# The first stage of a hybrid block kernel: c spread over partitions by its transfer, x times the first norm's factor by token and transposed a second time, first modulation on ScalarE

## The chip, the cores and the metric

The kernel runs on one core of a Trainium2 chip. The metric is the device time of one execution in microseconds, the median of the runs; lower is better. A core has five engines that run side by side, each through its own instructions in a fixed order: TensorE (PE in the profile, its weight loads PEld), VectorE (DVE), ScalarE (ACT), GpSimd (POOL) and SyncE (SP), which only starts transfers here. Transfers run on 16 DMA engines that all queues share.

## The reference

Two layers with three sub-blocks each (feed-forward, mixer, feed-forward) on x of 256 tokens by 1024, in fp32. Each sub-block begins with a norm that is modulated by a vector c. Only the first one matters here:

```python
c_act = jax.nn.silu(c)
mod = (c_act @ ada_w[layer] + ada_b[layer]).reshape(bsz, N_SUB, 3, D_MODEL)[:, :, :, None, :]

def rms_norm(x, g):
    y = xf * lax.rsqrt(jnp.mean(xf * xf, axis=-1, keepdims=True) + EPS)
    return y * g

def modulate(t, sub):
    return rms_norm(t, norm_g[layer, sub]) * (1.0 + mod[:, sub, 1]) + mod[:, sub, 0]

def swiglu(h, w_gate, w_up, w_down):
    return (jax.nn.silu(h @ w_gate) * (h @ w_up)) @ w_down

h = modulate(x, 0)
x = x + HALF_STEP * (1.0 + mod[:, 0, 2]) * swiglu(h, ...)
```

## The kernel before

Activations are kept with channels on the 128 partitions and the 256 tokens along the row: x is eight chunks of 128 by 256. Weights stream from memory once, in pieces of 128 by 1024, eight tiles each. To keep fp32 accuracy, each piece is split into a high part (a cast on ACT, `whi`, line 88 or 92) and the remainder (a subtraction on DVE, `wlo`, line 93), and each activation chunk likewise (`hb`, its two halves); a product is then three matmuls: high by high (line 309), high weight by low activation (310), low weight by high activation (311). Three buffers hold raw pieces, six the parts, three the raw ada blocks; a load waits on SP until its buffer is free.

In the first sub-block (`s == 0` in `ffn`) the loop runs over the eight chunks k of x on the outside, and for each over eight output blocks j, gate and up. So PE can begin with the first chunk alone: 48 matmuls for a chunk, into eight PSUM banks (four of tag `mm`, two `ax`, one `p`, one `q`). Ahead of that stand:

- **c** (lines 153 to 177): one row of 1024 is loaded from ACT's queue; PE spreads it over the partitions by a product with ones, in two halves of 512, and ACT applies Silu to each half, giving `cact`.
- **x** (lines 155 to 188): two loads on SP's queue, tokens on partitions (`xn`); DVE sums the squares of each half (line 182, with its sum in `ss_in`); PE transposes the sixteen 128 by 128 blocks (line 187), and ACT copies them to `x` (line 188), which is also what the residual adds to later.
- **the modulation** (`ada_block`, lines 199 to 207): each block is a load of 128 by 1024 on SP and a product with `cact` on DVE, summed along the row (line 206). Blocks 0 and 1 give shift and scale of chunk 0, and so on by pairs; those of chunk k + 1 are asked for while chunk k's products are issued. The columns of biases and gains (`cols`, line 451) come by ACT's queue, and `b1` (line 454), `scales` (458) and `shifts` (461) on DVE are made of them.
- **the norm's factor**: `rs_tokens` (263 to 276) makes of the two sums one factor for each token, in twelve small DVE steps (lines 275 and 252 to 259; the inverse root is an integer start and three Newton steps). `rs_bcast` (278 to 285) spreads it with PE to a row that is the same on all partitions, and ACT copies it to `rs`.
- **the chunk** (`modulate_chunk`, 319 to 328): DVE makes `ht`, x times scale times rs (line 323); ACT adds the shift and rounds to the high part (325); DVE makes the low part (326).

The order on each engine is fixed when the kernel is built, by a planner that takes instructions by their place in the program and by when it reckons them ready; it need not be the order of the lines. Some orders are set by hand: `W.first` holds the three instructions of the first chunk's modulation, and the first two weight remainders stand behind its first entry, the second high part behind its second:

```python
if i == 1:
    self.tc.add_manual_dep(raw_hi.ins, self.first[1].ins.name, NOSYNC, reason="the first input first")
...
if i < 2:
    self.tc.add_manual_dep(self.last.ins, self.first[0].ins.name, NOSYNC, reason="the first input first")
```

Of the kernel before, what the change touches and what calls it, by code (L numbers as in the profile page):

```python
# [11 lines left out]
F32 = mybir.dt.float32  # L12
F32R = mybir.dt.float32r
I32 = mybir.dt.int32
AF = mybir.ActivationFunctionType
ALU = mybir.AluOpType
# [3 lines left out]
P = 128  # L20
# [104 lines left out]
def body(ctx: ExitStack, tc: tile.TileContext, a, out, dbg=None):  # L125
# [14 lines left out]
    def mm_bank(name):  # L140
        return ps_mm.tile([P, 512], F32, tag="mm", name=name)
# [8 lines left out]

    first = ExitStack()
    fpool = first.enter_context(tc.tile_pool(name="first", bufs=1, reuse_waits="tile"))
    crow = fpool.tile([1, D], F32, name="crow")
    nc.scalar.dma_start(crow, a["c"])
    xn = fpool.tile([P, 2, D], F32, name="xn")
    nc.sync.dma_start(xn[:, 0], a["x"][0:P, :])
    nc.sync.dma_start(xn[:, 1], a["x"][P:T, :])
# [13 lines left out]
    ones = cst.tile([P, P], F32, name="ones")  # L171
    nc.gpsimd.memset(ones, 1.0)
    cact = cst.tile([P, D], F32, name="cact")
    for i in range(2):
        b = mm_bank(f"c{i}")
        nc.tensor.matmul(b, ones[0:1, :], crow[:, 512 * i:512 * i + 512], start=True, stop=True)
        nc.scalar.activation(cact[:, 512 * i:512 * i + 512], b, AF.Silu)

    ss_in = fpool.tile([P, 2], F32, name="ss_in")
    for b in range(2):  # L180
        q = fpool.tile([P, D], F32, name=f"xsq{b}")
        nc.vector.scalar_tensor_tensor(out=q, in0=xn[:, b], scalar=1.0, in1=xn[:, b], op0=ALU.mult, op1=ALU.mult,
                                       accum_out=ss_in[:, b:b + 1])
    for k in range(0, ND, 2):
        b = mm_bank(f"xT{k}")
        for i in range(4):
# [132 lines left out]
    def modulate_chunk(s, k, rs):  # L319
# [7 lines left out]
                                            in1=h[k][:, 0, :].bitcast(F32), op0=ALU.add, op1=ALU.subtract)  # L327
        return mul, hi, lo

    def scale_shift_columns(s):  # L330
        sh, _ = mod_shift_scale(s)
        shb = sh.unsqueeze(2).to_broadcast([P, 8, 2])
        nc.vector.tensor_copy(hh[:, :, T:T + 2], shb)
        nc.vector.tensor_tensor(out=hl[:, :, T:T + 2], in0=shb, in1=hh[:, :, T:T + 2].bitcast(F32), op=ALU.subtract)
# [93 lines left out]
    def ffn(s, acc, fp, during=None):  # L428
# [11 lines left out]
        if s == 0:  # L440

            done = NF0
            rs = xp.tile([P, T], F32, tag="rs", name="rs0")
            pb = rs_bcast(acc, D, "n0")
            nc.scalar.copy(rs, pb)
            banks = [mm_bank(f"gu0_{j}") if j < 4 else ax_bank(f"gu0_{j}", ("ax", "ax", "p", "q")[j - 4])
                     for j in range(NF0)]
            heads = [None] * NF0
# [8 lines left out]
            for k in range(ND):  # L457
                nc.vector.scalar_tensor_tensor(out=scales[0][:, k:k + 1], in0=mods[0][:, 8 + k:9 + k],
                                               scalar=b1[:, k:k + 1], in1=cols[:, g + k:g + k + 1],
                                               op0=ALU.add, op1=ALU.mult)  # L460
                nc.vector.tensor_tensor(out=shifts[0][:, k:k + 1], in0=mods[0][:, k:k + 1], in1=cols[:, o + k:o + k + 1],
                                        op=ALU.add)
                chain = modulate_chunk(0, k, pb if k == 0 else rs)
                if k == 0:
                    W.first = chain
                for j in range(NF0):
                    for i in range(2):
                        dst = banks[j][:, i * T:(i + 1) * T]

                        m = multiply(dst, h[k], k == 0 and i == 0, k == ND - 1)  # L470
                        if k == 0 and i == 0:
                            heads[j] = m
                        elif k == 0:
                            tc.add_manual_dep(m.ins, heads[j].ins.name, NOSYNC, reason="one start per bank")
                        if j == i == 0 and k + 1 < ND:
                            ada_block(2 * k + 2)
                            ada_block(2 * k + 3)
# [684 lines left out]
```

## Time and profile before

| | us |
|---|---|
| median of 3 runs | 1161.99 |
| lowest and highest | 1160.93, 1162.44 |
| the profiled execution | 1166.55 |
| its span, first to last instruction | 1164.6 |
| PE busy in it | 1139.7 |
| DVE busy in it | 960.0 |
| ACT busy in it | 640.8 |

The profile is of one execution. Its views used here are the page, the list of waits (engine, line, what it waited for: us in total, times, longest), the timeline (start, length, engine, line, operation, output and inputs, count, idle time before it and who ended it), groups by line (count, busy us, mean ns), and windows (length; busy us and count of PE, PEld, DVE, ACT and POOL; the granted clock of PE as a share of full; share of the DMA engines; GB/s). "SPq" and "ACTq" are the queues' issuing instructions.

### The profile page before, as it was taken

How to read it: one execution, taken by the hardware profiler on the slowest of the kernel's cores; microseconds unless marked ns; L12 is line 12 of the kernel's file. 1: busy time of each engine (PE TensorE's matmuls, PEld its weight loads, DVE VectorE, ACT ScalarE, POOL GpSimd, SP SyncE). 2: the span in 40 equal slices, each digit the busy share in tenths (PEclk: the TensorE clock that was granted, in tenths of full speed). 3: DMA queues.
4: the chain of work that ended last, by engine and by line, in shares of the span. 5: the costliest groups of instructions: out<-in, count | busy, mean ns of one | idle time of the engine just before them, and what ended most of it. 6: DMA issues, size and time to landing. Idle time of an engine off the chain costs nothing.

```text
span 1164.6 us, 21862 instructions
## 1 busy us (share of the span) xinstructions
PE 1139.7 (98%) x8526; PEld 1084.3 (93%) x8526; DVE 960.0 (82%) x1838; ACT 640.8 (55%) x1070; POOL 8.8 (1%) x24
## 2 busy tenths in 40 slices
PE   7999999999999999999999998999999999999997
PEld 6999988999988999998899998889999989999986
DVE  7999899999889798778788888979869988666553
ACT  4464444778875564444454354448765466444451
POOL 0000000000000000000000000010000000000000
PEclk8999999999999999999999999999999999999999
DMA  8989989556555568888748899973432475765550
GB/s 324 348 299 359 359 302 325 194 185 199 174 180 176 187 211 324 306 297 297 265 150 308 281 331 344 335 250 101 162 111 73 131 235 160 259 220 189 183 181 37
DMA packets 74985, 272.25 MB, mean 234 GB/s; under 512 B 8417, under 2 KB 8577, under 8 KB 74882
## 3 DMA queue, kind: packets, MB, share of 16 engines
q1 hardware_dynamic: 74016, 268.99, 67.6%
q8 instruction: 67, 1.10, 0.4%
q0 software_dynamic: 432, 1.10, 0.4%
q10 hardware_dynamic: 434, 0.76, 0.2%
q14 instruction: 36, 0.29, 0.1%
HBM read 269.77 MB, written 1.05 MB: 233 GB/s over the span
## 4 chain that ended last, share of the span: by engine, by line
PE 76%; DVE 11%; DMA 7%; ACT 3%; issue 1%; ACTq 0%; DVEq 0%; SPq 0%
PE od L410 16%; PE gu L310 11%; PE gu L311 11%; PE gu L309 11%; PE od L412 8%; DMA wraw<-in_wst_dram 5%; DVE wlo L93 4%; ACT whi L92 2%; DVE ada L206 1%; DMA wgr<-in_ml_wg_dram 1%; PE gu_f L358 1%; PE up L311 1%; PE up L310 1%; PE gu_f L356 1%; PE gu_f L357 1%
## 5 line engine op out<-in xcount | busy, mean ns | idle before, releaser
L92 ACT CAST whi<-wraw 128x1024 fp32r<-128x1024 f32 x364 | 380.4, 1048 | 304.2 <-DMA wraw<-in_wst_dram 151.0
L93 DVE TENSOR_TENSOR wlo<-wraw,whi 128x1024 fp32r<-128x1024 f32 x366 | 446.8, 1221 | 106.7 <-ACT whi L92 105.5
L311 PE MATMUL gu<-hb,wlo 128*128 128x256 f32 x1312 | 371.0, 284 | 0.0
L310 PE MATMUL gu<-hb,whi 128*128 128x256 f32 x1312 | 370.1, 283 | 0.1
L309 PE MATMUL gu<-hb,whi 128*128 128x256 f32 x1312 | 364.6, 282 | 1.5 <-ACT hb L325 1.5
L410 PE MATMUL od<-ph,whi 128*128 128x512 f32 x704 | 247.9, 395 | 3.3 <-DVE ph L303 3.3
L309 PEld LDWEIGHTS gu<-hb,whi 128*128 128x128 f32 x1312 | 248.7, 191 | 1.9 <-ACT hb L325 1.9
L310 PEld LDWEIGHTS gu<-hb,whi 128*128 128x128 f32 x1312 | 248.5, 189 | 0.4 <-DVE hb L326 0.3
L311 PEld LDWEIGHTS gu<-hb,wlo 128*128 128x128 f32 x1312 | 247.7, 189 | 0.0
L412 PE MATMUL od<-ph,wlo 128*128 128x256 f32 x704 | 197.6, 281 | 0.0
L206 DVE SCALAR_TENSOR_TENSOR ada<-ada,cact 128x1024 f32<-128x1024 f32 x144 | 175.0, 1218 | 0.0
L410 PEld LDWEIGHTS od<-ph,whi 128*128 128x128 f32 x704 | 133.0, 189 | 34.7 <-DVE ph L303 3.6
L412 PEld LDWEIGHTS od<-ph,wlo 128*128 128x128 f32 x704 | 132.7, 188 | 0.0
L302 ACT CAST ph<-fg 128x256 fp32r<-128x256 f32 x88 | 35.2, 405 | 87.2 <-DVE fg L437 86.9
L417 DVE SCALAR_TENSOR_TENSOR x<-od,gate,x 128x256 f32<-128x256 f32 x88 | 42.1, 481 | 26.8 <-PE od L412 22.1
L303 DVE TENSOR_TENSOR ph<-fg,ph 128x256 fp32r<-128x256 f32 x88 | 36.6, 421 | 12.6 <-ACT ph L302 12.5
L410 PE MATMUL od<-yb,whi 128*128 128x512 f32 x128 | 45.2, 395 | 0.0
L436 ACT ACTIVATE fg<-gu 128x256 f32<-128x256 f32 x82 | 30.8, 378 | 13.9 <-PE gu L311 13.8
L311 PE MATMUL zz<-hb,wlo 128*128 128x256 f32 x128 | 37.5, 293 | 0.0
L309 PE MATMUL zz<-hb,whi 128*128 128x256 f32 x128 | 37.5, 293 | 0.0
L310 PE MATMUL zz<-hb,whi 128*128 128x256 f32 x128 | 37.1, 290 | 0.0
L293 ACT ACTIVATE sq_o<-x 128x256 f32<-128x256 f32 x42 | 17.4, 415 | 35.1 <-DVE x L417 32.9
(398 smaller groups left out, 1882.8 us busy)
## 6 DMA issues: line engine op xcount, KB each, us to landing
wraw<-in_wst_dram SPq DMA_DIRECT2D x366, 512.0 KB, 4.4
ada<-in_adaT_dram SPq DMA_DIRECT2D x144, 512.0 KB, 5.4
xn<-in_x_dram SPq DMA_DIRECT2D x2, 512.0 KB, 4.0
wgr<-in_ml_wg_dram POOLq DMA_DIRECT2D x3, 256.0 KB, 6.4
out_dram<-res SPq DMA_DIRECT2D x2, 256.0 KB, 3.0
out_dram<-res ACTq DMA_DIRECT2D x2, 256.0 KB, 3.0
cols<-in_cols_dram ACTq DMA_DIRECT2D x1, 226.0 KB, 5.2
wkr<-in_ml_wkr_dram POOLq DMA_DIRECT2D x1, 128.0 KB, 3.5
```

Source lines behind the costliest of these rows:

```text
L92: raw_hi = nc.scalar.copy(hi, raw)
L93: self.last = nc.vector.tensor_tensor(out=lo, in0=raw, in1=hi.bitcast(F32), op=ALU.subtract)
L206: nc.vector.scalar_tensor_tensor(out=raw, in0=raw, scalar=1.0, in1=cact, op0=ALU.mult, op1=ALU.mult, accum_out=mods[s][:, m:m + 1])
L302: nc.scalar.copy(hi, src)
L303: nc.vector.tensor_tensor(out=both[:, 1, :], in0=src, in1=hi.bitcast(F32), op=ALU.subtract)
L309: m = nc.tensor.matmul(dst, wh, both[:, 0, :], start=start, stop=False, skip_group_check=True)
L310: nc.tensor.matmul(dst, wh, both[:, 1, :], start=False, stop=False, skip_group_check=True)
L311: nc.tensor.matmul(dst, wl, both[:, 0, :], start=False, stop=stop, skip_group_check=True)
L410: nc.tensor.matmul(bank, wh, both.rearrange("p i t -> p (i t)"), start=(k == 0), stop=False, skip_group_check=True)
L412: nc.tensor.matmul(sums[0], wl, both[:, 0, :], start=False, stop=(k == len(rhs) - 1), skip_group_check=True)
L417: nc.vector.scalar_tensor_tensor(out=xs_t[d], in0=part, scalar=g[:, d:d + 1], in1=xs_t[d], op0=ALU.mult, op1=ALU.add)
L436: nc.scalar.activation(g, b[:, 0:T], AF.Silu)
```

## The change

c is loaded as 128 copies of its row, 512 KB in place of 4 KB, straight into all partitions; the two products and the two half Silus become one Silu. The second half of x has its squares summed on ACT and not on DVE. The norm's factor is not spread to a row any more: x, with tokens on partitions, is multiplied by it in place (first half on ACT, second on DVE), and transposed a second time into a new tile `xr`, with ACT copying again. The first transposes, into `x`, stay for the residual. A chunk's modulation (`shift_chunk`) is two passes on ACT over `xr`, one rounded to the high part and one not, and one subtraction on DVE. It returns the subtraction first and the high part second, so the first two weight remainders now stand behind the low part.

```diff
-    crow = fpool.tile([1, D], F32, name="crow")
-    nc.scalar.dma_start(crow, a["c"])
+    call = fpool.tile([P, D], F32, name="call")
+    nc.scalar.dma_start(call, a["c"][0:1, :].to_broadcast([P, D]))
...
     cact = cst.tile([P, D], F32, name="cact")
-    for i in range(2):
-        b = mm_bank(f"c{i}")
-        nc.tensor.matmul(b, ones[0:1, :], crow[:, 512 * i:512 * i + 512], start=True, stop=True)
-        nc.scalar.activation(cact[:, 512 * i:512 * i + 512], b, AF.Silu)
+    nc.scalar.activation(cact, call, AF.Silu)
 
     ss_in = fpool.tile([P, 2], F32, name="ss_in")
-    for b in range(2):
-        q = fpool.tile([P, D], F32, name=f"xsq{b}")
-        nc.vector.scalar_tensor_tensor(out=q, in0=xn[:, b], scalar=1.0, in1=xn[:, b], op0=ALU.mult, op1=ALU.mult,
-                                       accum_out=ss_in[:, b:b + 1])
+    junk = [fpool.tile([P, D], F32, name=f"xsq{b}") for b in range(2)]
+    nc.vector.scalar_tensor_tensor(out=junk[0], in0=xn[:, 0], scalar=1.0, in1=xn[:, 0], op0=ALU.mult, op1=ALU.mult,
+                                   accum_out=ss_in[:, 0:1])
+    nc.scalar.activation(junk[1], xn[:, 1], AF.Square, accum_out=ss_in[:, 1:2])
...
+    def shift_chunk(k, src):
+
+        sh, sc = shifts[0], scales[0]
+        hi = nc.scalar.activation(h[k][:, 0, :], src, AF.Identity, bias=sh[:, k:k + 1], scale=sc[:, k:k + 1])
+        t = tmp.tile([P, T], F32, tag="v", name=f"ht0_{k}")
+        nc.scalar.activation(t, src, AF.Identity, bias=sh[:, k:k + 1], scale=sc[:, k:k + 1])
+        lo = nc.vector.tensor_tensor(out=h[k][:, 1, :], in0=t, in1=h[k][:, 0, :].bitcast(F32), op=ALU.subtract)
+        return lo, hi
...
-            rs = xp.tile([P, T], F32, tag="rs", name="rs0")
-            pb = rs_bcast(acc, D, "n0")
-            nc.scalar.copy(rs, pb)
+            rs = rs_tokens(acc, D, "n0")
+            xr = fpool.tile([P, ND, T], F32, name="xr")
+            for k in range(0, ND, 2):
+                w = slice(k * P, (k + 2) * P)
+                nc.scalar.activation(xn[:, 0, w], xn[:, 0, w], AF.Copy, scale=rs[:, 0:1])
+                nc.vector.tensor_scalar(out=xn[:, 1, w], in0=xn[:, 1, w], scalar1=rs[:, 1:2], scalar2=None,
+                                        op0=ALU.mult)
+                b = ax_bank(f"xr{k}", ("ax", "ax", "p", "q")[k // 2])
+                for i in range(4):
+                    nc.tensor.transpose(b[:, i * P:(i + 1) * P], xn[:, i % 2, (k + i // 2) * P:(k + i // 2 + 1) * P],
+                                        ident)
+                nc.scalar.copy(xr[:, k:k + 2, :], b.rearrange("p (k t) -> p k t", k=2))
...
-                chain = modulate_chunk(0, k, pb if k == 0 else rs)
+                chain = shift_chunk(k, xr[:, k, :])
```

## The prediction

> **What bounds the kernel now.** I read the page first: TensorE (PE) is busy nearly all of the span, so only time in which PE has nothing to do, or runs slowly, can be won. Then the list of waits for PE in the first 100 us, the stage that the change touches.
>
> ```profile
> span 1164.6 us, 21862 instructions
> PE 1139.7 (98%) x8526; PEld 1084.3 (93%) x8526; DVE 960.0 (82%) x1838; ACT 640.8 (55%) x1070; POOL 8.8 (1%) x24
> PE c L176 <- DMA crow<-in_c_dram: 2.9, 1, 2.9
> PE rsb_n L283 <- DVE rsy_n L259: 2.3, 1, 2.3
> PE gu L309 <- ACT hb L325: 1.5, 1, 1.5
> ```
>
> All of PE's waits in this stage lie before the first weight product. So I followed the start in the timeline (start, length, engine, line, operation).
>
> ```profile
> 2.95 3.75 PE L176 MATMUL c<-crow,ones 1*128 1x512 f32 x4 [2.95 <-DMA crow<-in_c_dram]
> 6.56 0.17 DVE L454 TENSOR_SCALAR b<-cols 128x8 f32<-128x8 f32 x1 [1.20 <-DMA cols<-in_cols_dram]
> 6.63 3.47 PE L187 MATMUL xT<-ident,xn 128*128 128x128 f32 x16
> 6.64 1.22 DVE L182 SCALAR_TENSOR_TENSOR xsq<-xn 128x1024 f32<-128x1024 f32 x1
> 7.90 0.17 DVE L275 TENSOR_SCALAR rsv_n<-ss_in 128x2 f32<-128x2 f32 x1
> 8.60 1.23 DVE L206 SCALAR_TENSOR_TENSOR ada<-ada,cact 128x1024 f32<-128x1024 f32 x1
> 10.02 1.22 DVE L206 SCALAR_TENSOR_TENSOR ada<-ada,cact 128x1024 f32<-128x1024 f32 x1
> 12.19 0.16 DVE L259 SCALAR_TENSOR_TENSOR rsy_n<-rsw_n,rsy_n 128x2 f32<-128x2 f32 x1
> 12.40 0.71 PE L283 MATMUL rsb_n<-ident,rsy_n 128*128 128x128 f32 x4 [2.31 <-DVE rsy_n L259]
> 13.56 0.48 DVE L323 SCALAR_TENSOR_TENSOR ht<-x,scale,rsb_n 128x256 f32<-128x256 f32 x1 [1.21 <-ACT rs L445]
> 13.95 1.22 DVE L93 TENSOR_TENSOR wlo<-wraw,whi 128x1024 fp32r<-128x1024 f32 x1
> 14.07 0.51 ACT L325 ACTIVATE hb<-ht,shift 128x256 fp32r<-128x256 f32 x1 [0.55 <-DVE ht L323]
> 14.63 1.52 PE L309 MATMUL gu<-hb,whi 128*128 128x256 f32 x5 [1.52 <-ACT hb L325]
> ```
>
> The path is VectorE (DVE): second square sum to 7.9, then the norm's twelve small steps with two ada blocks laid between them, to 12.35, then a relay PE, ACT, DVE, ACT of 2.3 us. The first product starts at **14.63**. It then runs on a halved clock, as the windows show (third number before the end: granted clock).
>
> ```profile
> 13.00:14.00 1.00, 0.12 (x2) 0.00 (x0) 0.44 (x2) 0.37 (x1) 0.00 (x0) 0.58 0.77 258
> 19.00:20.00 1.00, 1.00 (x7) 1.00 (x6) 0.96 (x4) 0.19 (x1) 0.00 (x0) 0.51 1.01 332
> 20.00:21.00 1.00, 1.00 (x10) 1.00 (x10) 1.00 (x2) 1.00 (x2) 0.00 (x0) 1.00 0.97 389
> 25.00:57.30 32.30, 32.30 (x273) 32.30 (x272) 32.07 (x55) 14.10 (x18) 0.00 (x0) 1.00 0.96 348
> ```
>
> The share of 0.58 puts the halving at about 13.2 (0.84 of that microsecond at half). From 14.63 to 20.0, 5.4 us at half speed, PE does 2.7 us of full-speed work. After that PE is full: from here the kernel ends when it ends whatever DVE does, unless a wait appears. I therefore reckon in the **full-speed start** of the product stream: now 14.63 + 2.7 = 17.3. Its shift is the change of the time.
>
> **What the change takes away is mostly off this path.** The c products (2.95 to 6.7) hold PE until the transposes at 6.63; without them the transposes wait for x instead. DVE loses 0.48 us (ht, L323) for each of eight chunks, and lo becomes a two-operand subtraction (0.42 by L303 for 0.48 by L326). DVE is busy 32.07 of 32.30 us there, but PE waits for it nowhere after 14.63, so I cost this at nothing; the weight stream that PE works through is the cover.
>
> **What it adds, step by step.**
>
> ```profile
> DMA to landing us min/median/max: 3.3/4.0/4.7
> DMA to landing us min/median/max: 5.9/6.3/6.7
> DMA to landing us min/median/max: 7.5/7.9/8.3
> 1.36 0.37 ACTq L451 DMA_DIRECT2D cols<-in_cols_dram  x1
> 2.65 0.99 SPq L83 DMA_DIRECT2D wraw<-in_wst_dram  x2
> 1.24 0.42 SPq L157 DMA_DIRECT2D xn<-in_x_dram  x1
> 1.71 0.90 SPq L204 DMA_DIRECT2D ada<-in_adaT_dram  x2
> cols<-in_cols_dram ACTq DMA_DIRECT2D x1, 226.0 KB, 5.2
> 6.00:7.00 1.00, 1.00 (x3) 0.38 (x3) 0.44 (x2) 0.27 (x1) 0.00 (x0) 1.00 1.03 418
> ```
>
> (The first three rows are for xn, for the first two ada loads and for the first two weight loads.) *Transfers.* The second half of x lands at 1.24 + 4.7 = 5.9, ada 0 and 1 at 7.6 and some 8.9. The engines are full at 418 GB/s, so 512 KB for c in place of 4 KB push all behind it by 0.524/0.41 = 1.3 us: x to 7.2, ada to 8.9 and 10.2. No row shows a wide transfer that reads one row 128 times; bounds are no delay (if x goes first) and, if it runs at a third of the rate, 3 us; I take the full rate, nearest to the x loads beside it. cols, behind c on ACT's queue, now lands at 1.36 + 5.2 = 6.6; sharing with x gives about 7.2. The loads queued on SP behind x move by the same 1.3 us: the first weight from 2.65 + 7.5 = 10.2 to 11.5, its cast on ACT (1.05) still done before the norm is.
>
> ```profile
> L759 ACT ACTIVATE lru_aq<-lru_aq 128x1024 f32<-128x1024 f32 x2 | 2.1, 1059 | 0.0
> L530 ACT ACTIVATE ena_lam<-ena_lam 128x8 f32<-128x8 f32 x1 | 0.2, 192 | 0.0
> L990 ACT ACTIVATE xc<-xc,cols 128x256 f32<-128x256 f32 x16 | 7.5, 510 | 1.9 <-PE s L878 1.8
> L188 ACT COPY x<-xT 128x512 f32<-128x512 f32 x4 | 2.3, 582 | 0.6 <-PE xT L187 0.5
> L506 ACT ACTIVATE lru_x<-xl,cols 128x256 f32<-128x256 f32 x8 | 4.5, 560 | 0.6 <-PE xl L311 0.6
> 1153.79 1.73 PE L1051 MATMUL fin<-ident,x 128*128 128x128 f32 x14
> L758 DVE TENSOR_SCALAR lru_aq<-lru_aq 128x1024 f32<-128x1024 f32 x2 | 1.4, 688 | 0.0
> L303 DVE TENSOR_TENSOR ph<-fg,ph 128x256 fp32r<-128x256 f32 x88 | 36.6, 421 | 12.6 <-ACT ph L302 12.5
> L326 DVE SCALAR_TENSOR_TENSOR hb<-ht,shift,hb 128x256 fp32r<-128x256 f32 x48 | 21.7, 481 | 1.7 <-ACT hb L325 1.6
> ```
>
> *Square sum on ACT.* Silu of c, 1.06 by the 1024-wide row, is over before x lands. The square then takes 7.2 + 1.06, and its accumulator between nothing and a smallest ACT operation, 0.19; I take 0.1: **8.4**, against 7.9. The square moves off DVE, yet x's landing binds it.
>
> *Norm on DVE.* Before 7.90 to 12.35, 4.45 us, of which two ada blocks take 2.6. I keep this order, add 0.2 for the later ada landings: 8.45 + 4.65 = **13.1**.
>
> *Relay to the first product.* Removed: the broadcast, rs and ht, 2.28 us in all with hi. In place of it: scaling x on ACT 0.51 (L990; DVE's half, a quarter of 0.69 by L758, is shorter), four transposes, copy 0.58 (L188), hi with scale and bias 0.56 (L506), and about 0.05 at each of five hand-overs. Four transposes at half clock with the last one's drain are 1.05 (sixteen took 3.47, 0.22 each; the clock column shows 1.00 there, but at the end of the kernel fourteen take 1.73, 0.12 each, so the earlier ones were at half). Sum 2.95. But ACT is in order: three more scalings (some 0.42 apart) and up to three more copies may stand ahead of hi, 1.6 us more. Between 2.95 and 4.55, I take 3.9, since in the code they all stand ahead of it: first product at **17.0**, 2.4 us later. The sixteen transposes fill PE meanwhile (3.5 us at half clock); if the order lets hi pass, twelve of them, 2.6 us, lie in the stream instead, so it comes out alike.
>
> *Clock.* Before, full speed came 5.4 us after PE's steady work began. Now the new transposes begin it at about 13.7 and end the halved stretch near 18.7, give or take a third of that. Of it the products see 1.7 us, costing 0.85 and not 2.7: gain 1.8.
>
> The page "TensorE: Matmul & The Clock Gate" of the Trainium skill (Part 1) has free-running windows of some 3.4 us and full clock after one busy window. Half clock from 13.2 to 20.0 here, 6.8 us, agrees with two such windows; by that rule the gain would differ from run to run by up to 3.4/2 = 1.7 us, and the sum would lie between nothing and +2.
>
> *Second operand.* The first weight remainders (wlo, L93) now queue behind lo and no longer behind ht: hi at 16.9, the second ACT pass 0.42 to 0.56, lo 0.42, then wlo 1.22, to about 19.1. PE has the high parts to multiply meanwhile, eight products of a weight piece at 0.21 each, then those with lo. Behind wlo the third weight load on SP waits for its buffer, and the ada loads for that: they are needed a chunk (5.7 us) later. Between nothing and 0.6; I take 0.2.
>
> **Sum:** +2.4 - 1.8 + 0.2 = **+0.8 us**. The profiled execution took 1166.55 (span 1164.6 with 1.95 around it) and would come to 1167.35; the median of the runs shown, 1161.99, is 4.6 lower, and the same shift on it gives **1162.8**. A measurement of this kernel tells about 0.2%, 2.3 us, from no change, so this is no change.
>
> **Rivals.** *The norm runs unbroken (faster).* If the ada blocks stand behind the twelve small steps, the factor is ready at 8.45 + 2.45 = 10.9; both ada blocks and the four DVE scalings then end near 14, hi lets the products start at 14.6, and PE has been at work since 11.5, so the clock is full by 16 or earlier: full-speed start 14.6 + 0.6 or less, 2.1 to 2.7 early, **1159.4**. For it: ada lands later than the square sum now. Against it: before, both blocks were put into the norm although they were not urgent.
>
> *cols comes late (slower).* b1 (L454) stood ahead of the norm in DVE's queue (6.56) and waits for cols, which now stands behind 512 KB in ACT's queue. Up to 8.4 that is free. From there each microsecond delays everything behind it; from 9.8 on it makes the kernel slower by over 0.2%. If the loads queued on SP take two turns for each of c's, or the one row is read at a third of the rate, cols lands at 10.5 or later: 2.1 us more and with the forecast +2.9, **1164.9**. Against it: the engines move 418 GB/s whatever the queue.
>
> The page "DMA: Bandwidth & Descriptors" of the Trainium skill (section "Latency and other measured facts") speaks against the change here: partitions that read at large power-of-two pitches dropped from 207 to 103 GB/s, by inference from many streams on one channel. One row for all partitions is the extreme of that; by half the rate c would take 5 us, and the sum would be +0.9 to +1.4. No run here shows such a transfer.
>
> *ACT holds the relay and the clock stays halved (slower).* First product at 17.65, full clock only at 20.5: +3.0 - 1.3 + 0.6, **1164.3**.
>
> *The change only moves work (no gain, no loss).* The relay equals what it replaces: **1162.0**.
>
> **How the numbers follow.** Forecast 0.50, nothing 0.15: same 0.65. Unbroken norm 0.13: faster. cols late 0.14, ACT and clock 0.08: slower 0.22. The range reaches from the unbroken norm, 1159.4, to late cols with the longest relay, 1164.9 + 0.65 + 0.6, about 1166.2.
>
> **What would show it.** Second half of x at 7.2; square on ACT to 8.4; ada between the norm's steps, its end at 13.1; first product at 17.0; half clock until about 18.7; no PE wait after that over 0.6. Wrong it is if cols lands after 8.4, if the norm ends by 11, or if PE waits for wlo or for a weight load in the second chunk (about 23 us).

## The result, and the profile after

| | kernel before | kernel after |
|---|---|---|
| median, us (9 runs each, same chip) | 1162.44 | **1168.34** |
| lowest to highest | 1160.93 to 1167.05 | 1166.21 to 1173.86 |
| profiled execution, and its span | 1166.55, 1164.6 | 1169.83, 1167.7 |

The ratio is 1.0044, with a 95% interval of 1.003 to 1.0058: the change makes the kernel slower, by some 5 us. That lies above the range that was forecast (1159.4 to 1166.2).

The page of after: PE is a little less busy, and DVE too.

```profile
span 1167.7 us, 21892 instructions
PE 1137.9 (97%) x8534; PEld 1085.0 (93%) x8534; DVE 956.5 (82%) x1832; ACT 648.7 (56%) x1086; POOL 8.7 (1%) x24
```

The start of after in the timeline (start, length, engine, line, operation, and in brackets the idle time before it with who ended it):

```profile
8.04 1.06 ACT L180 ACTIVATE xsq<-xn 128x1024 f32<-128x1024 f32 x1 [0.67 <-DMA xn<-in_x_dram]
8.52 0.17 DVE L470 TENSOR_SCALAR b<-cols 128x8 f32<-128x8 f32 x1 [1.23 <-DMA cols<-in_cols_dram]
9.01 0.19 ACT L180 ACTIVATION_READ_ACCUMULATOR xsq<-xn 128x1 f32 x1
9.56 1.23 DVE L204 SCALAR_TENSOR_TENSOR ada<-ada,cact 128x1024 f32<-128x1024 f32 x1 [0.86 <-DMA ada<-in_adaT_dram]
10.71 0.16 DVE L273 TENSOR_SCALAR rsv_n<-ss_in 128x2 f32<-128x2 f32 x1
13.94 0.16 DVE L257 SCALAR_TENSOR_TENSOR rsy_n<-rsw_n,rsy_n 128x2 f32<-128x2 f32 x1
14.14 1.31 ACT L454 ACTIVATE xn<-xn,rsy_n 128x256 f32<-128x256 f32 x3
14.70 2.82 PE L459 MATMUL xr<-ident,xn 128*128 128x128 f32 x12 [3.17 <-ACT xn L454]
15.85 0.59 ACT L461 COPY xr<-xr 128x512 f32<-128x512 f32 x1 [0.40 <-PE xr L459]
16.70 0.59 ACT L461 COPY xr<-xr 128x512 f32<-128x512 f32 x1 [0.27 <-PE xr L459]
17.56 0.58 ACT L461 COPY xr<-xr 128x512 f32<-128x512 f32 x1 [0.27 <-PE xr L459]
18.04 0.51 ACT L454 ACTIVATE xn<-xn,rsy_n 128x256 f32<-128x256 f32 x1
18.45 0.59 ACT L331 ACTIVATE hb<-xr,shift,scale 128x256 fp32r<-128x256 f32 x1
18.60 1.12 PE L459 MATMUL xr<-ident,xn 128*128 128x128 f32 x4 [1.08 <-ACT xn L454]
19.37 1.20 PE L307 MATMUL gu<-hb,whi 128*128 128x256 f32 x4
```

Read it from the bottom. The first product comes at 19.37, where before had it at 14.63. On PE it stands right behind the last four transposes (18.60), which wait for the fourth scaling (18.04), and the high part that it needs (L331, 18.45 to 19.04) stands behind that scaling on ACT. The scaling in turn stood on ACT behind three copies, each of which waits for PE's transposes. All this began when the norm ended (14.10). The norm's first step (L273) ran at 10.71 although its input was complete at 9.20: an ada block, whose transfer landed at 9.56, stood ahead of it in DVE's queue.

The windows of after (length; busy us and count of PE, PEld, DVE, ACT, POOL; granted clock; DMA share; GB/s):

```profile
3.00:4.00 1.00, 0.00 (x0) 0.00 (x0) 0.00 (x0) 0.01 (x1) 0.00 (x0) 1.00 0.85 303
4.00:5.00 1.00, 0.00 (x0) 0.00 (x0) 0.00 (x0) 0.00 (x0) 0.00 (x0) 1.00 0.78 299
20.00:21.00 1.00, 1.00 (x6) 1.00 (x6) 1.00 (x1) 1.00 (x2) 0.00 (x0) 1.00 0.82 299
22.00:23.00 1.00, 1.00 (x8) 1.00 (x8) 1.00 (x2) 1.00 (x3) 0.00 (x0) 1.00 0.86 164
23.00:24.00 1.00, 1.00 (x11) 1.00 (x10) 1.00 (x3) 0.22 (x1) 0.00 (x0) 1.00 0.86 340
381.00:384.00 3.00, 2.95 (x14) 2.95 (x15) 3.00 (x6) 1.11 (x2) 0.00 (x0) 0.52 0.50 184
```

While c is transferred (3 to 5 us) the engines move 300 GB/s. PE starts 6 products in a microsecond at 20 and 11 at 23: half pace until about 22.7. (The clock column shows 1.00 there, because the record holds no event of the clock before that one.) And at 381 the clock is halved again, in the second sub-block (the hybrid stage). The list of PE's waits shows what stands before that:

```profile
PE xr L459 <- ACT xn L454: 4.3, 2, 3.2
PE od L307 <- ACT ylb L300: 2.3, 1, 2.3
PE od L417 <- DVE ph L301: 1.5, 1, 1.5
...
PE dtT L585 <- DVE shc_bc L378: 1.3, 1, 1.3
```

The first is in the start above. The others are in later stages, at 378 us (ylb), 728 (od, L417) and 222 (dtT).

### The profile page after: what moved, and what is told of

Same layout as the page of the kernel before. It is cut to its first block, busy times and chain, and to the rows that moved or that the text cites. A ratio compares the mean times of both kernels' runs of the same rounds, so it can differ in the third digit from the quotient of the medians.

```text
span 1167.7 us, 21892 instructions
## 1 busy us (share of the span) xinstructions
PE 1137.9 (97%) x8534; PEld 1085.0 (93%) x8534; DVE 956.5 (82%) x1832; ACT 648.7 (56%) x1086; POOL 8.7 (1%) x24
## 4 chain that ended last, share of the span: by engine, by line
PE 84%; DVE 8%; DMA 4%; ACT 3%; issue 1%; SPq 0%; DVEq 0%; POOL 0%; ACTq 0%
PE od L417 16%; PE gu L308 13%; PE gu L309 13%; PE gu L307 13%; PE od L419 8%; DVE wlo L93 2%; DMA wraw<-in_wst_dram 2%; ACT whi L92 1%; PE up L309 1%; PE gu_f L365 1%; PE gu_f L363 1%; PE up L308 1%; PE gu_f L364 1%; PE up L307 1%; PE od L307 1%
## 5 line engine op out<-in xcount | busy, mean ns | idle before, releaser
L417 PE MATMUL od<-ph,whi 128*128 128x512 f32 x704 | 246.3, 393 | 1.5 <-DVE ph L301 1.5
L417 PEld LDWEIGHTS od<-ph,whi 128*128 128x128 f32 x704 | 132.2, 188 | 32.5 <-DVE ph L301 1.8
L417 PE MATMUL od<-yb,whi 128*128 128x512 f32 x128 | 45.2, 395 | 0.0
L419 PE MATMUL od<-yb,wlo 128*128 128x256 f32 x128 | 36.0, 283 | 0.0
```

The costliest lines, as they stand in the source:

```text
L417: nc.tensor.matmul(bank, wh, both.rearrange("p i t -> p (i t)"), start=(k == 0), stop=False, skip_group_check=True)
L419: nc.tensor.matmul(sums[0], wl, both[:, 0, :], start=False, stop=(k == len(rhs) - 1), skip_group_check=True)
```

## The experiments

Most figures here are shifts of marks along the program, from the rows of each trace: the start of the 400th product of the first stage, and the ends of the last `dtT` product (early in the hybrid stage), of the last `od<-ylb` product (the stage's last), of the last `od<-ph` product of the fourth sub-block, and of the span. They are given against a second profile of the kernel before (e0_before_again), in us; its own marks are in the first row. The last column is the ratio to the kernel before on the same chip, with its 95% interval.

| kernel | 400th | dtT | ylb | 4th | end | median | ratio |
|---|---|---|---|---|---|---|---|
| e0_before_again | (64.24) | (231.59) | (399.15) | (775.53) | (1158.42) | 1161.77 | 0.9994 (0.9979 to 1.0008) |
| before, first profile | 0.5 | 0.8 | 1.2 | 6.3 | 6.2 | | |
| e1_c_only | 3.0 | 3.0 | 3.0 | 3.1 | 3.3 | 1163.68 | 1.0001 (0.9989 to 1.0013) |
| e2_x_only | 1.7 | 4.8 | 7.0 | 6.9 | 6.8 | 1167.13 | 1.0029 (1.0014 to 1.0045) |
| after | 4.3 | 5.5 | 7.5 | 9.3 | 9.3 | 1168.34 | 1.0044 (1.003 to 1.0058) |
| e11_after_again | 4.3 | 4.7 | 6.4 | 8.2 | 8.2 | 1167.38 | 1.0049 (1.0032 to 1.0066) |
| e3_rows | 4.1 | 5.8 | 6.0 | 6.0 | 6.0 | 1166.67 | 1.003 (1.0015 to 1.0046) |
| e4_first_chunk | 3.1 | 4.0 | 6.7 | 8.1 | 7.9 | 1168.01 | 1.0037 (1.0022 to 1.0052) |
| e5_square | 1.5 | 2.0 | 2.1 | 6.5 | 6.6 | 1162.19 | 0.9989 (0.9972 to 1.0005) |
| e6_pad | 1.6 | 2.9 | 2.5 | 2.5 | 2.6 | 1164.23 | 1.0017 (1.0005 to 1.003) |
| e7_overlay | 5.3 | 6.4 | 6.7 | 6.7 | 6.8 | 1166.50 | 1.0034 (1.002 to 1.0048) |
| e12_x_overlay | 3.2 | 3.3 | 3.9 | 3.9 | 3.7 | 1163.88 | 1.0017 (1.0007 to 1.0028) |
| e9_norm_first | 4.2 | 5.5 | 6.8 | 7.0 | 6.7 | 1167.33 | 1.0047 (1.0029 to 1.0065) |
| e14_repaired | 2.1 | 2.2 | 3.1 | 3.9 | 4.0 | 1164.63 | 1.0017 (1.0009 to 1.0026) |
| e10_warm | -0.2 | -0.1 | -0.3 | 0.2 | 0.1 | 1160.60 | 0.9991 (0.9979 to 1.0002) |
| e13_warm_norm | -1.8 | -1.8 | -2.2 | -1.0 | -1.0 | 1161.00 | 0.9983 (0.9974 to 0.9992) |

One row is one execution, so a single step in it can be chance; the median is of 6 to 12. The second profile of before is one of its fastest executions (1160.30 against a median of 1161.77), so the column of the end lies mostly 1 to 4 us above what the ratios say.

### The parts alone, and the start

**e1_c_only:** the kernel before, with c spread by its transfer and nothing else.

```diff
-    crow = fpool.tile([1, D], F32, name="crow")
-    nc.scalar.dma_start(crow, a["c"])
+    call = fpool.tile([P, D], F32, name="call")
+    nc.scalar.dma_start(call, a["c"][0:1, :].to_broadcast([P, D]))
...
+    nc.scalar.activation(cact, call, AF.Silu)
```

> The kernel before with only the first part of the change: c spread by its transfer and one Silu; squares, norm, relay and first modulation as before. Transfer theory (the 512 KB at the head are what costs): second half of x lands near 8.0 us, the norm ends near 14.1, first product near 16.4, the time 1 to 2.5 us over before. Relay theory (the scalings, second transposes and copies ahead of the first product are what costs): first product within 0.5 us of 14.6, the time within 0.5 us of before.

The first product comes at 17.09, and the 400th 3.0 us late, so c alone costs the start more than the forecast gave the whole change. The median moves by 1.1 only, and the interval holds no change. But the fastest executions are 1163.05 against 1160.08 of before, which is the 3.0 again. The first profile of before lost some 5 us at 722 us (below), its executions run up to 1168.55, and no wait of that kind stands in the profile of e1_c_only. Whether such losses hide the 3.0 in the median, and whether c's later start or chance keeps them away, was not settled.

**e2_x_only:** all of the change but c, which is spread by PE as before.

```diff
-    call = fpool.tile([P, D], F32, name="call")
-    nc.scalar.dma_start(call, a["c"][0:1, :].to_broadcast([P, D]))
+    crow = fpool.tile([1, D], F32, name="crow")
+    nc.scalar.dma_start(crow, a["c"])
...
+        nc.tensor.matmul(b, ones[0:1, :], crow[:, 512 * i:512 * i + 512], start=True, stop=True)
```

> The change without its first part: c is one row, spread by products with ones, as before; all the rest as in the changed kernel. Relay theory: x lands at 5.9, the norm ends near 12.2, the relay takes 5.2 us, first product near 17.4, the time 2 to 3.5 us over before. Transfer theory: first product by 15.5, the time within 1 us of before.

The start loses only 1.7 us, yet the hybrid stage loses 5.3 more. That part was in no sum. The starts of the two parts nearly add up (3.0 + 1.7, against 4.3 in both profiles of after).

**e3_rows:** after, with c's 128 partitions filled from 128 different rows of the same size (the block adaT[0]; c's values are replaced, so the modulation differs).

```diff
-    nc.scalar.dma_start(call, a["c"][0:1, :].to_broadcast([P, D]))
+    nc.scalar.dma_start(call, a["adaT"][0])
```

> The changed kernel, but c's 128 partitions are filled from 128 different rows (an ada block) in place of 128 times the same row: the same bytes, the same queue, the same order; the modulation is computed from other numbers. If reading one row 128 times is what slowed the transfers between 3 and 6 us (some 300 GB/s): second half of x lands near 7.2 and not 8.0, first product 0.8 us earlier, time about 0.8 us under the changed kernel. If it is the bytes and the turns of two queues alone: landings and time as in the changed kernel within 0.3 us.

The windows of e3_rows:

```profile
3.00:4.00 1.00, 0.00 (x0) 0.00 (x0) 0.00 (x0) 0.01 (x1) 0.00 (x0) 1.00 1.00 406
4.00:5.00 1.00, 0.00 (x0) 0.00 (x0) 0.00 (x0) 0.00 (x0) 0.00 (x0) 1.00 1.03 414
```

406 and 414 GB/s here, 303 and 299 in after. The transposes that need the second half of x start at 7.49 instead of 8.07. So of the 2.1 us by which x came later than in before, about 0.6 come from reading one row 128 times, and the rest from the bytes. The first product comes 0.8 earlier than in after (18.59), the 400th only 0.2, and the ratio is not told apart from after's. This kernel has after's order and its tiles lie as in after, yet its PE waits 1.3 us for ylb and nothing at 728 us, and no clock is halved there: behind the `dtT` mark it loses 0.2 us, where after loses 3.8.

**e4_first_chunk:** after, with the first chunk's modulation issued after one pair's scaling, transposes and copy, ahead of the other three pairs.

```diff
-            for k in range(0, ND, 2):
+            def relay(k):
...
+            relay(0)
...
                 if k == 0:
                     W.first = chain
+                    for q in (2, 4, 6):
+                        relay(q)
```

> The changed kernel with the first chunk's modulation written ahead of the scalings, transposes and copies of the other three pairs of chunks. Relay theory: the high part no longer waits for the fourth scaling, first product at 17.3 to 18.0 in place of 19.4, time 1 to 2 us under the changed kernel. If the start of the products doesn't decide (what is lost lies in later stages): the time of the changed kernel within 0.5 us.

The first product comes at 17.9, 3.7 us after the norm's end (14.2) and not 5.3, and the 400th 1.2 us earlier than in after. The time doesn't follow: 1168.01, and the interval, over 3 us wide, can't tell 1.2 us. In its profile the waits for ylb (3.1 us, with a halved clock behind it) and at 728 us (1.1) come again: 4.8 us are lost behind the 400th product, 5.0 and 3.9 in the two profiles of after.

**e5_square:** the kernel before, with the second half's squares on ACT.

```diff
-        nc.vector.scalar_tensor_tensor(out=q, in0=xn[:, b], scalar=1.0, in1=xn[:, b], op0=ALU.mult, op1=ALU.mult,
-                                       accum_out=ss_in[:, b:b + 1])
+        if b == 0:
...
+        else:
+            nc.scalar.activation(q, xn[:, b], AF.Square, accum_out=ss_in[:, b:b + 1])
```

> The kernel before with the second half's squares on ACT alone. The list scheduler then puts the first modulation block ahead of the norm's first step on DVE. If the scheduler's order costs what it cost in the kernel after (the norm's step waits for that block's transfer and runs behind it), the norm ends within 0.7 us of where it ends in the kernel before, since the square that left DVE (1.2 us) makes room for the block (1.2 us): first product at 14.0 to 15.3 us, time 1162.6 us within 0.7. If the move of the squares is worth what it frees, the first product comes at 13.4 us and the time is 1161.4.

The first product at 14.54 and the norm's end at 12.26 are where they were (14.97 and 12.18 in the second profile of before). The planner puts the ada block ahead of the norm here too, but its transfer is early without c's, so the swap costs nothing.

### The hybrid stage

**e0_before_again:** the kernel before, unchanged.

> The kernel before once more, unchanged, for a second profile of it. All theories: 1162.6 us within 0.1%. If the profiled execution of before was an unusually long one, the second profile has a span of 1159 to 1161 us, its stretch from 600 to 690 us is 3 to 5 us shorter than in the first, and the lapse of the clock at 726 us is gone. In the hybrid stage (200 to 390 us) PE's waits for DVE shc_bc stay under 0.5 us and the longest for ACT ylb stays under 1.5 us if these belong to the kernel; if they are a matter of chance, one of them is over 2.

Its span is 1158.4. The execution on which the forecast was made had lost 5 us at 722 us: PE waited 3.3 us there, and its clock was halved for 3.4 us after it. The second profile has neither, and so it is the one to compare with. Its PE waits 1.3 us at most for ylb and nothing for shc_bc.

**e6_pad:** the kernel before, with a tile of 8 KB per partition, which nothing reads, among the first ones. The order on every engine stays as it is.

```diff
+    pad = fpool.tile([P, ND, T], F32, name="pad")
+    nc.gpsimd.memset(pad[:, 0, 0:1], 0.0)
```

> The kernel before, with an unused tile of the size of xr (8 KB per partition) among the first tiles: the order of instructions on every engine stays as it is, only the places of later tiles in memory move. Theory 'start' (the change costs what its start costs): 1162.6 us, as before. Theory 'places' (the loss in the hybrid stage comes from tiles that lie elsewhere, so that their loads wait for other readers): 1164.6 to 1166.6 us, with the waits of PE for DVE shc_bc at 1.2 us, for ACT ylb over 2 us and a lapse of the clock behind it. Theory 'chance' (which transfer lands late in the hybrid stage differs from one execution to the next): 1162.6 us.

An unused tile makes the kernel slower by 0.17% (0.05 to 0.3). The timeline of e0_before_again:

```profile
201.29 0.67 POOL L559 DMA_DIRECT2D hv<-in_ssd_hv_dram  x1 [199.57 <-PE od L412]
207.38 1.28 ACT L583 ACT_TABLE_LOAD   x1
208.68 0.22 ACT L583 ACTIVATE hv<-hv 128x16 f32<-128x16 f32 x1
```

and of e6_pad:

```profile
204.32 0.67 POOL L561 DMA_DIRECT2D hv<-in_ssd_hv_dram  x1 [202.57 <-PE od L414]
211.30 1.28 ACT L585 ACT_TABLE_LOAD   x1 [2.30 <-DMA hv<-in_ssd_hv_dram]
212.60 0.21 ACT L585 ACTIVATE hv<-hv 128x16 f32<-128x16 f32 x1
```

`hv` is a small constant of the hybrid stage, loaded from POOL's queue into memory that the first stage used. By the profile its load waits for an `od` product; that this is the last one that reads the place is read from the kernel, since a trace holds no addresses. In before it goes out 3.2 us ahead of the hybrid stage's first `bc` product (204.45); with the pad `hv` lies elsewhere, and goes out 1.8 us ahead of it (206.09). The next weights are asked for 2.0 us behind it in before and 0.6 us with the pad. The list of transfers has, for e0_before_again and for e6_pad (KB each, us from issue to landing):

```profile
hv<-in_ssd_hv_dram POOLq DMA_DIRECT2D x1, 16.0 KB, 3.9
```

```profile
hv<-in_ssd_hv_dram POOLq DMA_DIRECT2D x1, 16.0 KB, 6.9
```

ACT waits 2.3 us for it, with the casts of weights and the activations for PE queued behind, and PE waits for dtT:

```profile
PE dtT L571 <- DVE shc_bc L373: 1.3, 1, 1.3
```

after has a wait of the same length at the same place, but not by the same way. The timeline of after:

```profile
214.02 1.05 ACT L92 CAST whi<-wraw 128x1024 fp32r<-128x1024 f32 x1 [2.30 <-DMA wraw<-in_wst_dram]
215.75 1.28 ACT L599 ACT_TABLE_LOAD   x1
217.04 0.22 ACT L599 ACTIVATE hv<-hv 128x16 f32<-128x16 f32 x1
```

Here too hv takes long (6.1 us), but it has landed at 213.1, and ACT reads it only at 217.04: ACT's wait is 2.30 us for a weight load. The planner has laid the hybrid stage of after in another order than that of before, with one more cast of weights (214.02) and that of `wdh` ahead of hv. e3_rows, e7_overlay and e11_after_again have after's order there; e2_x_only, e4_first_chunk, e9_norm_first and e14_repaired read hv ahead of that cast, as before does. The other 1 us of e6_pad came at the start of its profile (first product 15.85, 400th 1.6 late), and its cause was not followed.

**e7_overlay:** after, with xr laid over the two tiles that take the squares, which nothing reads. Order as in after, places as in before.

```diff
-    junk = [fpool.tile([P, D], F32, name=f"xsq{b}") for b in range(2)]
+    xr = fpool.tile([P, ND, T], F32, name="xr")
+    junk = [xr[:, 4 * b:4 * b + 4, :].rearrange("p k t -> p (k t)") for b in range(2)]
```

> The kernel after, with xr laid over the two tiles that take the squares (they are never read): same order of instructions, places in memory as in the kernel before. Theory 'start': 1168.3 us, as after. Theory 'places': 1163.5 to 1166 us, with PE's waits in the hybrid stage as in the kernel before (under 0.5 us for DVE shc_bc, under 1.5 us for ACT ylb, no lapse of the clock at 380 us). Theory 'order' (the list scheduler puts the hybrid stage's instructions in another order): 1168.3 us, with the wait for DVE shc_bc at 1.3 us still there.

1166.50 lies between the theories, and the ratio is not told apart from after's. PE's wait for shc_bc is 0.5 us, that for ylb 1.2, no halved clock at 380, none at 728: from the 400th product on this execution loses 1.5 us, after 5.0 and 3.9. But e3_rows, with xr in a place of its own, loses only 1.9 there, so this profile doesn't tell the places from chance. The 400th product came a microsecond later than after's, although the clock was full from 18.11 and not from 22.7: PE waited 1.4 us for hb between 55 and 69 us, where ACT waited 4.7 us for a weight load.

**e12_x_overlay:** e2_x_only with the same overlay.

> e2_x_only (the x part of the change alone, 1167.1 us) with xr laid over the two tiles of squares: same order of instructions, places in memory as in the kernel before. Theory 'places': the wait of PE for DVE shc_bc falls from 1.2 us to under 0.5, ACT's wait for hv goes, and the time is 1164 to 1165.3 us. Theory 'x relay': 1167.1 us, the hybrid stage still loses 3 us or more.

1163.88, a little under what theory "places" had, though the 400th product came 1.5 us later than in e2_x_only: the norm ended at the same time (12.3 and 12.4), but the clock was full from 22.33 and not from 15.81. The load of hv lands 3.7 us after its issue and not 6.8, PE's wait for shc_bc is 0.2 us and not 1.2, and behind the 400th product 0.5 us are lost, in e2_x_only 5.1. The order of instructions is the same in both. The two ratios overlap in their intervals; it is the steps in the profiles that show the difference.

**e11_after_again:** after, unchanged.

> The kernel after once more, unchanged, for a second profile of it: 1168.3 us within 0.1%. The start (first product 19.4 us, 400th product 4.3 us behind that of the second profile of before) and PE's wait for DVE shc_bc (1.2 us) come again if they belong to the kernel. The lapse of the clock after the wait for ACT ylb (2.0 us with the wait) comes again if it belongs to the kernel; if it is a matter of chance it is missing, as it was in the profile of e3_rows, and the span is 2 us or more shorter than 1167.7.

The start repeats to 0.05 us. The wait for ylb (2.4 us) and the halved clock behind it come again, and so does the wait at 728 us (1.5). The wait for shc_bc is 0.5 this time.

### The order at the start

**e9_norm_first:** after, with the first two ada blocks held behind the norm's last step.

```diff
-            ada_block(0)
-            ada_block(1)
+            for b in range(2):
+                tc.add_manual_dep(ada_block(b).ins, rsqrt_ends[0].ins.name, NOSYNC, reason="the norm first")
```

> The kernel after, with the first two modulation blocks held behind the norm's last step on DVE. Theory 'the block was put ahead': the norm no longer waits for the block's transfer (9.56 us) and runs unbroken from the second square's sum (9.2 us): it ends near 11.6 us instead of 14.1, the first product comes at 16.7 to 17.5 us instead of 19.37, and the time falls by about 2 us, to 1166.0 to 1166.5. Theory 'only the transfers count': the norm ends at 13.3 us or later and the time is within 0.7 us of 1168.3.

The norm ends at 11.59, as expected, and the first product comes at 19.48, no earlier than in after. The timeline of e9_norm_first says why:

```profile
16.59 0.59 ACT L331 ACTIVATE hb<-xr,shift,scale 128x256 fp32r<-128x256 f32 x1
18.38 1.99 ACT L88 CAST whi<-wraw 128x1024 fp32r<-128x1024 f32 x2
19.48 0.58 PE L307 MATMUL gu<-hb,whi 128*128 128x256 f32 x1 [1.62 <-ACT whi L88]
```

The high part came 1.9 us earlier, but the planner, reckoning anew, had moved the cast of the first weights (18.38, two pieces) behind the relay (in after it ran at 12.04). One link was mended and the next one held, and the time (1167.33, ratio 1.0047) is that of after.

**e14_repaired:** after with its start ordered by hand (norm first, the cast ahead of the copies, the first chunk ahead of the other three copies), and the overlay.

```diff
...
+            for b in range(2):
+                tc.add_manual_dep(ada_block(b).ins, rsqrt_ends[0].ins.name, NOSYNC, reason="the norm first")
...
+                        if k == j == i == 0:
+                            for r in relay[1:]:
+                                tc.add_manual_dep(r.ins, chain[0].ins.name, NOSYNC, reason="the first chunk first")
+                            tc.add_manual_dep(relay[0].ins, W.splits[0][0].ins.name, NOSYNC, reason="whi first")
```

> The kernel after with its start ordered by hand: the norm ahead of the modulation blocks, the cast of the first weights ahead of the copies of the second transposition, the first chunk's modulation ahead of the other three copies, and xr laid over the tiles of squares. Theory 'order and places': the first product comes at 16.3 to 17.3 us instead of 19.4, the 400th product 2 to 2.6 us behind that of the second profile of before instead of 4.3, the wait for DVE shc_bc falls under 0.6 us, and the time is 1163.5 to 1165 us. Theory 'the relay itself': what is gained at the first product is lost again before the 400th (which comes 4 us or more behind), and the time is 1166 us or more.

```profile
16.86 0.74 PE L308 MATMUL gu<-hb,whi 128*128 128x256 f32 x4 [0.49 <-ACT hb L332]
```

First product at 16.86, 400th 2.1 us late, 1164.63: theory "order and places". The same work in another order, with xr in another place, recovers most of the loss: the ratio is 1.0017 where after had 1.0044 and 1.0049, some 3.4 of some 5.4 us. What is left in its profile is the start's 2.1 us, and 0.9 at ylb and 0.8 behind it. No run has the ordered start without the overlay, so the two aren't told apart here; and with this start the planner also gives the hybrid stage the order of before.

**e10_warm:** the kernel before, with 16 transposes of the identity that keep PE busy until the first product: ten behind the transposes of x, six behind the norm's rows.

```diff
+    wb = ax_bank("warm", "q")
+    for i in range(NWARM):
+        wt = nc.tensor.transpose(wb[:, 0:P], ident, ident)
...
+            for i in range(6):
+                wt = nc.tensor.transpose(wb[:, 0:P], ident, ident)
...
```

> The kernel before, with 16 transposes of the identity into an unused bank between the transposes of x and the first product, so that TensorE is busy from 6 us on. Theory 'clock': in the second profile of before the granted clock is full from 18.49 us, while the first product is at 14.97, so 3.5 us run at half pace and cost 1.76 us (2.7 in the first profile); with TensorE busy earlier the clock is full before 15 us, the 200th product comes 1.7 to 2.7 us earlier, and the time is 1159.5 to 1160.5 us. Theory 'the start does not reach the end': 1162 us. If the extra transposes hold up the norm's rows (12.2 us) the first product is later by what they hold: within 0.5 us.

The timeline of e10_warm:

```profile
8.77 1.82 PE L188 MATMUL xT<-ident,xn 128*128 128x128 f32 x8
10.43 1.26 PE L193 MATMUL warm<-ident 128*128 128x128 f32 x10
15.07 0.62 PE L316 MATMUL gu<-hb,whi 128*128 128x256 f32 x3 [0.86 <-ACT hb L332]
```

Ten transposes take 1.26 us, where eight took 1.82: the clock is full from about 10.4, not 18.5. In this execution the row of c landed 1.0 us later than in the second profile of before and the norm ended 0.6 later, and still the 200th product came 0.4 earlier (1.7 to 2.7 were expected). So the clock is worth about 1 us by this estimate, not the 1.76 that half pace costs: among its first hundred products PE at full pace waits 0.5 us for hb and whi, and in before it waits for nothing there. The median is 1.1 lower, the interval holds no change.

**e13_warm_norm:** e10_warm with the ada blocks behind the norm.

> e10_warm with the first two modulation blocks held behind the norm's last step on DVE. Theory 'order at the start': the norm runs unbroken and ends near 10.5 us instead of 12.2 to 12.8, the first product comes at 13.8 to 14.3 us instead of 15.0, and the time is 1159.5 to 1160 us against 1160.6 of e10_warm. Theory 'the blocks are needed just as much': the first modulation waits for the second block, which ends no earlier, the first product comes at 15 us and the time is 1160.6 us.

The timeline of e13_warm_norm:

```profile
9.79 0.16 DVE L265 SCALAR_TENSOR_TENSOR rsy_n<-rsw_n,rsy_n 128x2 f32<-128x2 f32 x1
11.02 1.22 DVE L211 SCALAR_TENSOR_TENSOR ada<-ada,cact 128x1024 f32<-128x1024 f32 x1
12.62 0.48 DVE L330 SCALAR_TENSOR_TENSOR ht<-x,scale,rsb_n 128x256 f32<-128x256 f32 x1
13.70 0.74 PE L316 MATMUL gu<-hb,whi 128*128 128x256 f32 x4 [1.24 <-ACT hb L332]
```

The norm ends at 9.95, the relay over PE and ACT runs beside the second ada block, and the first product comes at 13.70. The ratio to before is 0.9983 (0.9974 to 0.9992): the one version whose interval lies under the kernel before, by 2 us. The median of 1161.00 is above the 1159.5 to 1160 expected, on a chip where before has 1162.68; from e10_warm it is not told apart.

## Why the prediction was wrong

Two steps failed. The start was summed to +0.8 us and moved by 3.7 on the forecast's own measure, the full-speed start. And what comes behind the start was costed at nothing and lost 3.9 to 5.0 us more. Point by point, after's first profile:

| step | predicted | measured |
|---|---|---|
| second half of x lands | 7.2 | 8.04 |
| cols lands | 7.2 | 8.5 |
| second square sum complete | 8.4 | 9.20 |
| first step of the norm | 8.45 | 10.71 |
| end of the norm | 13.1 | 14.10 |
| relay to the first product | 3.9 | 5.27 |
| first product | 17.0 | 19.37 |
| full clock | 18.7 | 22.7 |
| full-speed start | 18.1 | 21.0 |
| loss behind the start | 0 | 3.9 to 5.0 |

**The transfer** was mis-sized. "I take the full rate": 512 KB at 0.41 MB/us gave 1.3 us, and x came 2.1 later. The bound of a third of the rate had held it. The page "DMA: Bandwidth & Descriptors" of the Trainium skill (section "Latency and other measured facts") tells of rows at large power-of-two pitches that ran at half rate. One row for all partitions is not the case that it measured. Here the engines moved 300 of 410 GB/s while it ran, so it slows, by a quarter and not by half. The prediction's 5 us "by half the rate" go with the 103 GB/s that it names; half of 0.41 MB/us gives 2.6.

**The norm** began 2.3 us late. "I keep this order": the ada blocks stayed between the steps, but one of the two had gone ahead of the first step, where it waits for a transfer that c had delayed to 9.56. In e5_square the same order without c's transfer cost nothing, so it is the two together. That block was then gone from between the steps, so the end was only 1.0 late. cols landed at 8.5, past the 8.4 that the forecast had named as a sign of being wrong, but it held nothing: DVE waited for the ada block's transfer after it.

**The relay** of 3.9 is right where the first chunk goes first (e4_first_chunk: 3.7). The upper bound of 4.55 counted ACT's queue as work alone. In after ACT's three copies each wait for PE at half pace (0.40, 0.27 and 0.27 idle), and the fourth scaling, planned behind them, holds the last four transposes. A bound on an in-order queue must count what its entries wait for.

**The clock** was to be full 2 us after the first product, as "the sixteen transposes fill PE meanwhile". (By its own terms, 13.7 and 5.4, that would be 19.1 and not 18.7.) PE stood still 3.17 us before them and 1.08 among them, and the clock stayed halved to 22.7. The rival "ACT holds the relay and the clock stays halved" was the mechanism of the start, but with 17.65 and 20.5 for 19.37 and 22.7. The page "TensorE: Matmul & The Clock Gate" of the Trainium skill (Part 1) has full clock after one busy window of some 3.4 us; the traces agree: 22.7 is 3.3 behind 19.37, and in e10_warm, with PE busy from 7, it is full at 10.4. But the moment isn't fixed by the order: e7_overlay has the same order and the same idle stretches (3.19 and 1.14 us), and its clock is full from 18.11, ahead of its first product (19.09).

The gain of 1.8 us was also mis-sized, whenever the clock comes. From the first to the hundredth product PE takes 14.32 us in the profile that the forecast used (halved for 5.35), 13.50 in after (halved for 3.3) and 12.84 in e7_overlay (not halved). So a halved start cost some 1.5 us in before and not 2.7, and 0.7 in after and not 1.7: at full pace PE loses part of it again, 0.4 us of it in e7_overlay in waits for hb and whi.

**What comes behind the start** was to cost nothing: "Its shift is the change of the time", and of the rest "I cost this at nothing; the weight stream that PE works through is the cover". A start's shift alone does stay: e1_c_only has 3.0 us at the 400th product and 3.3 at the end. (Of a gain some is lost: e13_warm_norm has 1.8 and 1.0.) But the change does more than move the start, in two ways that the runs show.

Its new tile moves later tiles that share memory with the first ones. In the seven profiles in which xr or the pad has a place of its own, the load of hv goes out 1.8 us ahead of the hybrid stage's first `bc` product and takes 5.8 to 6.9 us; in the other nine it goes out 3.2 us ahead and takes 3.5 to 4.4. Where ACT reads hv ahead of its next cast (e2_x_only, e4_first_chunk, e6_pad, e9_norm_first), ACT then waits 2.0 to 2.3 us and PE 0.9 to 1.3. By the ratios the moved places are worth 2.0 us in e6_pad (0.6 to 3.5) and 1.4 from e2_x_only to e12_x_overlay, where the intervals overlap.

And the planner gave after another order in the hybrid stage, in which ACT doesn't wait for hv but for a weight load: PE waits 1.3 and 0.5 us for shc_bc in the two profiles of after, and 0.5 in e7_overlay, which has the places of before. So what the places cost after itself is not shown.

The rest of the later loss is the wait for ylb with its halved clock (2.0 and 1.7 us in the profiles of after) and the wait at 728 (1.8 in both). The wait for ylb follows one weight load, the one asked for at 373.32 in after. It takes 5.0 to 6.4 us in the six profiles in which the clock is halved there (e2_x_only, e4_first_chunk, e9_norm_first, e14_repaired and both of after), and 4.2 to 4.8 in the other ten. e3_rows is among the ten, with after's order and places, so neither decides it alone. Why that load is late stays open, and so does the wait at 728. So does the wait at 722 us in the kernel before, which struck in two (before, e5_square) of the seven profiles of kernels that have its order and tiles there or nearly so.

It struck the very execution that the forecast used. With 1166.55 against a median of 1162, that could be seen, and the forecast laid only the shift on the median, so this did no harm to it. It would have hidden 5 us of a comparison of the two first profiles, whose ends lie only 3.1 us apart.

## What to carry to other kernels

When a change adds a tile, look at what shares its memory in later stages: which loads wait there for a last reader, and what is queued behind them. A bound for a step on an in-order engine needs the waits of the entries ahead of it, not only their lengths, and a planner that reckons anew may move an instruction that you did not touch. Before comparing two profiles, take a second one of the kernel before and lay marks along the program: where the difference steps, look there for a wait or a halved clock, and in a third profile whether it comes again.

## What the runs showed of the hardware

A short wait can cost PE more than itself. In the 16 profiles, each idle stretch of PE of 1.9 us or more behind the start (1.9, 2.3, 2.3, 2.45, 2.6, 3.1 and 3.3 us, seven in all) was followed by 3.4 us of halved clock, which began at most 1.4 us after its end. Of three stretches of 1.5 us one was; of those up to 1.34 us none was. At 722 us in before, the 3.3 us of waiting and half of the 3.4 make up the 5.1 us lost there; at ylb in after, 2.3 us and the halved clock cost 2.0 against the second profile of before, which waits 1.3 there itself. The Trainium skill's page "TensorE: Matmul & The Clock Gate" (Part 1) names an idle window of some 3.4 us: here 1.9 were enough, and the halved stretch has that length.

While one row was read into 128 partitions, the engines moved 300 GB/s in all, and 406 to 414 with 128 rows in its place. And the load of 16 KB took 3.5 to 4.4 or 5.8 to 6.9 us to land, by the instant at which it was issued among the weights.
